# Weight sums by accumulating DMA: a later start in the unit table, oldest token first, the accumulation one loop turn behind its plain copy, and two GpSimd splits moved to VectorE

## The chip, the cores and the metric

The kernel runs on one core of one Trainium2 chip. The metric is device time in microseconds, from the first to the last instruction of the slowest core, here the only one. The profile is one execution of the same program, recorded by the hardware profiler.

## The reference, cut to what matters

One layer of a diffusion backbone, batch 1, 1024 latent tokens, width 1024, 256 context tokens. Two attention branches work on the same modulated tokens: A, windowed (each block of 128 queries sees at most 3 blocks of keys and the context, with a sink logit per head), and B, global (1024 + 256 keys). Each has 8 heads in 2 key groups. Their outputs are projected, gated, merged, and a ConvFFN follows:

```
proj = h @ w_in + b_in
o_a  = windowed_attention(q_a, k_a, v_a, k_ctx, v_ctx, sink)
o_b  = global_attention(q_b, [k_b, k_ctx], [v_b, v_ctx])
y    = (sigmoid(ga) * (o_a @ w_branch_a) + sigmoid(gb) * (o_b @ w_branch_b)) @ w_out
x    = layer_norm(alpha * x + gate1 * y)
u    = depthwise_conv3(h2 @ w_up)
y    = (silu(u_gate) * u_val) @ w_down
out  = layer_norm(alpha * x + gate2 * y)
```

The last product, with `w_down`, is done by a seven-product scheme on 2 x 2 blocks. It needs four sums of blocks of `w_down`, which are weights: they depend on nothing that the kernel computes.

## The kernel before, in words

Everything is float32 in two parts (a rounded high part and the rest), so a product is three matmuls (`mm3`, lines 88 to 91) or two where one operand is exact. The stages follow each other: modulation and projections, the gates, attention, merge and output projection with the first LayerNorm, the FFN up products, the down products with the second LayerNorm.

**Attention units.** The loop over `u` (0 to 32) goes over 32 units: units 0 to 15 are branch A (`br` 0), 16 to 31 are branch B (`br` 1). Unit `br_i_g` is query block `i` and key group `g`; tiles carry this in their names (`ptl_3_0_3` is of unit i=3, g=0). In a unit:

- `qprep` (two units ahead): GpSimd splits the queries into `qs` (lines 83, 86), TensorE transposes them (line 483), ScalarE copies to `q1`, and SyncE swaps halves by two DMAs `q<-q` (lines 487, 488).
- `lat`: TensorE makes the scores (lines 493, 494), VectorE `p` (line 538), ScalarE the exponential (line 505).
- `rows` (line 577 and after): the reciprocal row sums go to a small DRAM tile `dn` (DMA `dn<-rb`, line 586), and come back spread over partitions (two DMAs `rb<-dn`, line 588). The DRAM tag of each `dn` tile is put on a list, `tokens`.
- `tr_step`: TensorE transposes 128 x 512 of `p` to PSUM (`ptr`, line 614), ScalarE writes the high part `pth` (line 623), VectorE the low part `ptl` (line 624). For the key tiles in `POOL_LO` (tile 3 in branch A, 2 and 6 in B) the split is *pooled*: ScalarE copies `ptr` to `prw` (line 620), and GpSimd makes `pth` and `ptl` (lines 83, 86).
- `av_step`: two matmuls with `pth` and `ptl` (lines 635, 636).
- `out_step`: ScalarE copies `avs` (line 641), GpSimd `up` (line 643), VectorE or GpSimd `ot` (line 647), GpSimd multiplies by `rb` (line 650) and splits the result to `O` (lines 83, 86).

**The sums.** `DNS` (line 65) tells after which unit `wd_sums` is called, with which sum (`n`) and which blocks (`j0` to `j1`; 4, 4 and 3 of 11). Each call of `put` takes a tag from `tokens`, makes a DRAM tile `sd` with that tag, so that the tile's DMAs stand behind the `dn` tile that had the tag, fills it by a plain DMA on SyncE's queue (1 MB, or 768 KB for the last three blocks), and adds one more block by an accumulating DMA on GpSimd's queue (line 685). Sums 1 and 3 start from weights alone. Sum 2 starts as a copy of the finished sum 1, sum 4 as a copy of the finished sum 2. So a block group has 4 plain and 4 accumulating DMAs, and all three groups have 12 and 12.

**What sets the order.** In the attention stage no order is written out: a list scheduler with a cost model of its own emits each engine's instructions when their inputs and buffers are free, by the order of the program among those that are ready. An engine, SyncE and GpSimd among them, then works its list strictly in that order. A DMA instruction with a wait holds up all that stands behind it on its engine.

Of the kernel before, what the change touches and what calls it, by code (L numbers as in the profile page):

```python
# [10 lines left out]
ALU = mybir.AluOpType  # L11
# [7 lines left out]
NT = 8  # L19
# [9 lines left out]
POOL_LO = (3,), (2, 6)  # L29
# [32 lines left out]
VOFF = 0.0  # L62
VSPAN = 1.0
VSC = 0, 1
DNS = {u0 + 2 * n + (u0 == 20): (n, j0, j1) for u0, j0, j1 in ((16, 0, 4), (20, 4, 8), (24, 8, 11)) for n in range(3)}


@with_exitstack
def layer_kernel(
# [6 lines left out]
    nc = tc.nc  # L76
    PSUM = bass.MemoryType.PSUM

    def split(src, hi, lo, hi_eng, lo_eng):
        if hi_eng is nc.scalar:  # L80
            nc.scalar.copy(hi, src)  # L81
        elif hi_eng is nc.gpsimd:
            nc.gpsimd.tensor_scalar(out=hi, in0=src, scalar1=1.0, scalar2=0.0, op0=ALU.mult, op1=ALU.add)
        else:
            hi_eng.tensor_copy(hi, src)
        lo_eng.tensor_tensor(out=lo, in0=src, in1=hi.bitcast(F32), op=ALU.subtract)  # L86
# [376 lines left out]
    class Unit:  # L463
# [141 lines left out]
        def value_steps(self):  # L605
            nm, kt = self.id, self.kt
            vh = self.br * 2 + self.g
            last = self.id == f"1_{NT - 1}_1"
            parts = {}

            def tr_step(n):
                tr = pt_tile(f"ptr{nm}_{n}")
                for h in range(4):
                    nc.tensor.transpose(tr[:, h * P:(h + 1) * P], self.pslice(h, n), ident)  # L614
                hi = att.tile([P, 512], R32, tag="pth", name=f"pth{nm}_{n}", bufs=4)
                lo = att.tile([P, 512], R32, tag="ptl", name=f"ptl{nm}_{n}", bufs=4)
                pooled = n in POOL_LO[self.br] and not last
                if pooled:
                    rw = att.tile([P, 512], F32, tag="ptr", name=f"prw{nm}_{n}", bufs=2)
                    nc.scalar.copy(rw, tr)  # L620
                    split(rw, hi, lo, nc.gpsimd, nc.gpsimd)
                else:
                    nc.scalar.copy(hi, tr)  # L623
                    nc.vector.tensor_tensor(out=lo, in0=tr, in1=hi.bitcast(F32), op=ALU.subtract)  # L624
                parts[n] = hi, lo
                return pooled

            def av_step(n):
                first = self.left == len(kt)
                self.left -= 1  # L630
                if first:
                    self.av = ps2.tile([P, 512], F32, tag="av", name=f"av{nm}")
                hi, lo = parts.pop(n)
                v = VT[kt[n] // 2][:, kt[n] % 2, vh]
                nc.tensor.matmul(self.av, v, hi, start=first, stop=False)  # L635
                nc.tensor.matmul(self.av, v, lo, start=False, stop=self.left == 0)  # L636

            def out_step():
                av = self.av
                avs = att.tile([P, 512], F32, tag="ptr", name=f"avs{nm}", bufs=2)  # L640
                nc.scalar.copy(avs, av)  # L641
                up = att.tile([HD, 512], F32, tag="up", name=f"up{nm}", bufs=1)
                nc.gpsimd.tensor_scalar(out=up, in0=avs[HD:P], scalar1=1.0, scalar2=0.0, op0=ALU.mult, op1=ALU.add)
                ot = att.tile([P, 2, P], F32, tag="ot", name=f"ot{nm}", bufs=1)
                oe = nc.gpsimd if self.br and not last else nc.vector
                for h in range(2):
                    oe.tensor_tensor(out=ot[h * HD:(h + 1) * HD],
                                     in0=avs[0:HD].rearrange("p (a b q) -> p a b q", b=2, q=P)[:, :, h],
                                     in1=up.rearrange("p (a b q) -> p a b q", b=2, q=P)[:, :, h], op=ALU.add)
                nc.gpsimd.tensor_tensor(out=ot, in0=ot, in1=self.rb, op=ALU.mult)  # L650
                hf = self.i // 4
                qs = slice((self.i % 4) * P, (self.i % 4 + 1) * P)
                split(ot, otile(self.br, hf, 0, self.g)[:, :, qs], otile(self.br, hf, 1, self.g)[:, :, qs],
                      nc.gpsimd, nc.gpsimd)

            def step(ns):
                pooled = [tr_step(n) for n in ns]
                for n, pl in zip(ns, pooled):
                    clk[0] += 1
                    avq.append((self, n, clk[0] + LAG[self.br] + (PLAG[self.br] if pl else 0)))  # L660
                    av_issue()

            self.left = len(kt)
            self.av_step, self.out_step = av_step, out_step
            g = 1 + self.br
            steps = [lambda n=n: step(range(n, n + g)) for n in range(0, len(kt), g)]
            steps.insert(3 if self.br else 2 if self.i else len(steps), self.rows)
            return steps

    tokens = []  # L670
    sd = {}

    def wd_sums(n, j0, j1):
        def a(r, c):
            return w_dn[c * NH + j0:c * NH + j1][:, :, 4 * r:4 * r + 4].rearrange("n p f q -> p n (f q)")

        def put(key, src, *more):
            tag = tokens.pop()
            t = dpool.tile([P, j1 - j0, HALF], F32, tag=tag, name=f"sd{key}_{j0}")
            for j in range(j0, j1):  # L680
                sd[key, j] = t[:, j - j0]
            sd[key] = t
            nc.sync.dma_start(t, src)
            for m in more:
                nc.gpsimd.dma_start(t, m, accum_op=ALU.add)

        if n == 0:
            put(1, a(1, 0), a(1, 1))
            put(3, a(0, 0), a(1, 0))
        elif n == 1:  # L690
            put(2, sd[1], a(0, 0))
        else:
            put(4, sd[2], a(0, 1))
# [130 lines left out]
    for n, (gi, k) in enumerate(order):  # L824
# [8 lines left out]
        if gi == "g":  # L833
            for hf in (0, 1):
                last = gate(k, hf)
# [50 lines left out]
    def otile(br, hf, hl, g):  # L886
        key = br, hf, hl, g
        if key not in O:
            O[key] = opool.tile([P, 2, HALF], R32, tag="O", name="O%d%d%d%d" % key, bufs=12)
        return O[key]  # L890
# [4 lines left out]
    def pt_tile(name, dt=F32):  # L895
        return ps2.tile([P, 512], dt, tag="pt", name=name, bufs=3)
# [17 lines left out]
    def av_issue(flush=False):  # L914
        while avq:
            u = avq[0][0]
            c = [e for e in avq if e[0] is u and (flush or e[2] <= clk[0])]
            if not c:
                return
            e = min(c, key=lambda e: e[2])  # L920
            avq.remove(e)
            u.av_step(e[1])
            if u.left == 0:
                u.out_step()
# [36 lines left out]
    def done(br, i, g):  # L961
        if g and i % 2:
            hput(f"Q{br}_{i - 1}")
        if g and i == NT - 1:
            hput(f"KL{br * 2}", f"KL{br * 2 + 1}")
# [4 lines left out]
    for u in range(nu + 1):  # L970
        vs, fs = [], []
        while vq and (vq[0] <= u - VL or vq[0] >= 16 or u >= 17):
            vs += units[vq.pop(0)].value_steps()
        ss = []
        if u < nu:
            ss = units[u].score_steps()
            if u + 2 < nu:
                ss.append(units[u + 2].qprep)
        if u == 31:
            first = branch_steps(1, w_b, (0, 1), att, (nc.gpsimd, nc.gpsimd), (0,))  # L980
            first[0]()
        for hf, (u0, u1) in enumerate(FILL):
            if u == u0:
                fill += branch_steps(0, w_a, (hf,), att, (nc.gpsimd, nc.gpsimd))
                ends = [n * (u1 - u0) / len(fill) for n in range(len(fill))]
            if u0 <= u < u1:
                fs = [fill.pop(0) for e in ends if u - u0 <= e < u - u0 + 1]
        if u < nu:
            ss = [units[u].context] + ss
        seq = []  # L990
        for lst, of, sp in ((ss, 0.0, SPAN[u >= 17]), (vs, VOFF, VSPAN), (fs, 0.0, 1.0)):
            for n, st_ in enumerate(lst):
                seq.append((of + sp * (n + 0.5) / len(lst), st_))
        for _, st_ in sorted(seq, key=lambda e: e[0]):
            st_()
        if u in DNS:
            wd_sums(*DNS[u])
        if u < nu:
            vq.append(u)
            done(units[u].br, units[u].i, units[u].g)  # L1000
# [86 lines left out]
    for f in range(2, KT):  # L1087
# [4 lines left out]
        for hs in halves:  # L1092
            n = HALF * len(hs)
# [239 lines left out]
    for f in (4, 6):  # L1333
        for si in (1, 2):
# [3 lines left out]
            elif f == 6:  # L1338
                (_, st), (_, dg), (_, ca), *ap = ln1(si)
                n = len(pend) - 4  # L1340
# [584 lines left out]
```

## Time and profile before

| | us |
|---|---|
| median of 3 runs (1563.13 to 1565.62) | 1564.17 |
| the profiled execution | 1565.22 |
| its span, first to last instruction | 1563.4 |
| TensorE (PE) busy in the span | 1531.6 |
| VectorE (DVE), ScalarE (ACT), GpSimd (POOL) busy | 1187.6, 808.6, 782.2 |
| branch A units, about | 336 to 466 |
| branch B units, about | 458 to 756 |
| plain DMAs of the sums issued | 458.4 to 686.1 |
| accumulating DMAs of the sums issued | 465.7 to 692.3 |

In a row of the timeline the first number is the start in us from the span's start, the second the duration in us; a bracket at its end is the idle time of that engine just before, and what ended it. "POOL L685" is GpSimd's issue of an accumulating DMA, "SPq L683" SyncE's issue of a plain one. In a row of the windows view each engine's busy us in the stretch is followed by its number of instructions; then come the granted TensorE clock, the mean busy share of the 16 DMA engines, and GB/s.

### The profile page before, as it was taken

The numbers are of one execution on the slowest core, as the hardware profiler recorded it, in microseconds if no ns is written. First come the engines' busy times: TensorE is split into PE (matmuls) and PEld (weight loads), VectorE is DVE, ScalarE is ACT, GpSimd is POOL, SyncE is SP. The second block draws the span as 40 slices with busy tenths as digits, with TensorE's granted clock in tenths as the row PEclk, the third lists the DMA queues.
The fourth block names the chain that finished last, engine by engine and source line by source line (L and its number), as shares of the span: only waits on it lengthen the run. The fifth ranks groups of instructions, "written<-read, shape, count | busy, mean of one in ns | idle before, by whom it ended". The sixth has DMA issues, their size and how long they took to land.

```text
span 1563.4 us, 22286 instructions
## 1 busy us (share of the span) xinstructions
PE 1531.6 (98%) x7804; PEld 1282.2 (82%) x7804; DVE 1187.6 (76%) x1714; ACT 808.6 (52%) x1431; POOL 782.2 (50%) x795
## 2 busy tenths in 40 slices
PE   9999999999999999999999999999999999999997
PEld 7888888888877877877888997888888888888887
DVE  6677976548887777777774788888888888657884
ACT  5322223358887777777431673544444444435552
POOL 0356422526666777776332455666677764121121
PEclk9999999999999999999999999999999999999998
DMA  9776662322235666631550223233334446996721
GB/s 371 267 239 239 207 245 92 106 84 66 65 116 137 150 149 151 148 80 35 180 184 16 98 79 120 81 112 115 120 102 114 113 117 191 363 265 212 251 103 55
DMA packets 113105, 232.11 MB, mean 148 GB/s; under 512 B 13056, under 2 KB 27904, under 8 KB 112896
## 3 DMA queue, kind: packets, MB, share of 16 engines
q1 hardware_dynamic: 97760, 201.82, 38.4%
q0 software_dynamic: 10400, 20.19, 8.3%
q10 hardware_dynamic: 4832, 8.68, 1.5%
q8 instruction: 61, 1.00, 0.3%
q14 instruction: 52, 0.43, 0.1%
HBM read 179.45 MB, written 65.86 MB: 157 GB/s over the span
## 4 chain that ended last, share of the span: by engine, by line
PE 54%; DVE 3%; ACT 1%; issue 1%; POOL 0%; DVEq 0%; ACTq 0%
PE p L89 4%; PE p L90 4%; PE p L91 4%; PE b L89 2%; PE b L91 2%; PE b L90 2%; PE c L89 2%; PE c L91 2%; PE d L91 2%; PE d L89 2%; PE c L90 2%; PE d L90 2%; PE a L91 2%; PE a L89 2%; PE a L90 2%; PE y L91 2%
## 5 line engine op out<-in xcount | busy, mean ns | idle before, releaser
L624 DVE TENSOR_TENSOR ptl<-ptr,pth 128x512 fp32r<-128x512 f32 x190 | 126.2, 682 | 32.6 <-ACT pth L623 32.2
L623 ACT CAST pth<-ptr 128x512 fp32r<-128x512 f32 x190 | 108.0, 593 | 54.0 <-PE ptr L614 32.6
L86 DVE TENSOR_TENSOR ld<-rd,hd 128x1024 fp32r<-128x1024 f32 x77 | 94.9, 1249 | 50.2 <-ACT hd L81 48.1
L505 ACT ACTIVATE p<-p,nm 128x1024 f32<-128x1024 f32 (+2 forms) x128 | 125.9, 985 | 4.5 <-DVE p L538 4.3
L614 PE MATMUL ptr<-ident,p 128*128 128x128 f32 x816 | 122.4, 277 | 4.4 <-DVE ptl L624 3.2
L81 ACT CAST hd<-rd 128x1024 fp32r<-128x1024 f32 x77 | 79.5, 1050 | 81.1 <-PE p L91 55.1
L614 PEld LDWEIGHTS ptr<-ident,p 128*128 128x128 f32 x816 | 94.1, 141 | 25.6 <-DVE ptl L624 7.9
L86 POOL TENSOR_TENSOR wlg<-wg,whg 128x512 fp32r<-128x512 f32 x32 | 47.7, 1500 | 123.3 <-ACT whg L81 123.3
L635 PE MATMUL av<-pth,VT 128*128 128x512 f32 x236 | 104.6, 443 | 2.1 <-ACT avs L641 1.5
L89 PE MATMUL p<-hd 128*128 128x512 f32 x264 | 103.2, 391 | 0.0
L91 PE MATMUL p<-hd,ld 128*128 128x512 f32 x264 | 102.7, 389 | 0.0
L90 PE MATMUL p<-ld,hd 128*128 128x512 f32 x264 | 102.7, 389 | 0.0
L636 PE MATMUL av<-ptl,VT 128*128 128x512 f32 x236 | 98.1, 416 | 2.7 <-POOL ptl L86 2.7
L89 PE MATMUL g<-hh,whg 128*128 128x512 f32 x256 | 99.9, 390 | 0.0
L91 PE MATMUL g<-hh,wlg 128*128 128x512 f32 x256 | 99.7, 389 | 0.0
L90 PE MATMUL g<-hl,whg 128*128 128x512 f32 x256 | 99.6, 389 | 0.0
L538 DVE TENSOR_SCALAR_CACHE_REDUCE p<-s,cvt,nmc 128x1024 f32<-128x1024 f32 x64 | 83.2, 1316 | 8.8 <-PE s L494 7.7
L493 PE MATMUL s<-KL,q 128*128 128x512 f32 (+2 forms) x192 | 75.6, 394 | 5.3 <-ACT p_x L505 2.8
L787 ACT ACTIVATE sg<-g,bgc 128x512 f32<-128x512 f32 x32 | 22.0, 686 | 96.1 <-PE g L91 96.1
L494 PE MATMUL s<-KL,q 128*128 128x512 f32 (+2 forms) x192 | 71.6, 373 | 0.0
L81 ACT CAST wS<-s 128x512 fp32r<-128x512 f32 x76 | 45.3, 620 | 46.4 <-POOL s L1227 45.7
L81 ACT CAST wA<-ru 128x512 fp32r<-128x512 f32 x57 | 35.5, 623 | 62.4 <-PE d L91 33.8
(436 smaller groups left out, 5015.2 us busy)
## 6 DMA issues: line engine op xcount, KB each, us to landing
wml<-in_wmodT_dram SPq DMA_DIRECT2D x48, 512.0 KB
ru<-in_w_up_dram SPq DMA_DIRECT2D x38, 512.0 KB
rd<-td SPq DMA_DIRECT2D x55, 256.0 KB
rd<-sd SPq DMA_DIRECT2D x44, 256.0 KB
rd<-in_w_dn_dram SPq DMA_DIRECT2D x33, 256.0 KB
wm<-in_wmodT_dram SPq DMA_DIRECT2D x16, 512.0 KB
wg<-in_w_g_dram SPq DMA_DIRECT2D x32, 256.0 KB
sgd<-sg ACTq DMA_DIRECT2D x32, 256.0 KB
```

What stands on the lines that cost most here:

```text
L81: nc.scalar.copy(hi, src)
L86: lo_eng.tensor_tensor(out=lo, in0=src, in1=hi.bitcast(F32), op=ALU.subtract)
L89: nc.tensor.matmul(ps, a[0], b[0], start=start, stop=False, skip_group_check=resumed)
L90: nc.tensor.matmul(ps, a[0], b[1], start=False, stop=False, skip_group_check=resumed)
L91: nc.tensor.matmul(ps, a[1], b[0], start=False, stop=stop, skip_group_check=resumed)
L505: nc.scalar.activation(p, s, AF.Exp, bias=nm[:, h:h + 1], scale=scale, accum_out=sm[:, h:h + 1])
L538: nc.vector.tensor_scalar(out=p, in0=o, scalar1=self.qscale(nqs)[:, hs] if self.br else -1.0, scalar2=self.other[:, hs], op0=ALU.mult, op1 ...
L614: nc.tensor.transpose(tr[:, h * P:(h + 1) * P], self.pslice(h, n), ident)
L623: nc.scalar.copy(hi, tr)
L624: nc.vector.tensor_tensor(out=lo, in0=tr, in1=hi.bitcast(F32), op=ALU.subtract)
L635: nc.tensor.matmul(self.av, v, hi, start=first, stop=False)
L636: nc.tensor.matmul(self.av, v, lo, start=False, stop=self.left == 0)
```

## The change

Four edits:

```diff
-DNS = {u0 + 2 * n + (u0 == 20): (n, j0, j1) for u0, j0, j1 in ((16, 0, 4), (20, 4, 8), (24, 8, 11)) for n in range(3)}
+DNS = {u0 + 2 * n + (u0 == 22): (n, j0, j1) for u0, j0, j1 in ((18, 0, 4), (22, 4, 8), (26, 8, 11)) for n in range(3)}
...
-                pooled = n in POOL_LO[self.br] and not last
+                pooled = n in POOL_LO[self.br] and not last and self.id[:3] != f"0_{NT - 1}"
...
     tokens = []
+    adds = []
...
-            tag = tokens.pop()
+            tag = tokens.pop(0)
...
             nc.sync.dma_start(t, src)
-            for m in more:
-                nc.gpsimd.dma_start(t, m, accum_op=ALU.add)
+            adds.extend((t, m) for m in more)
...
         for _, st_ in sorted(seq, key=lambda e: e[0]):
             st_()
+        while adds:
+            t, m = adds.pop(0)
+            nc.gpsimd.dma_start(t, m, accum_op=ALU.add)
         if u in DNS:
             wd_sums(*DNS[u])
```

The table calls each sum two units later. The accumulating DMA of a sum stands in the program one turn of the unit loop behind its plain DMA. The tag is the oldest on the list and no longer the newest. And in units 0_7_0 and 0_7_1, the last two of the first branch, branch A, tile 3 is split by ScalarE and VectorE and not by GpSimd.

The table and the program say "later"; what the scheduler makes of it is another matter, since the newest token at unit 16 was that of a unit just done, and the oldest at unit 18 is that of unit 0. The first place is SyncE's list in the first units of branch A (`sd_0_6091` is sum 2 of the first blocks, `sd_0_6546` their sum 4, `dn` and `rb` the row sums, `q` the swapped queries, `bT` a gate load):

```order
+L684 DMA sd_0_6091<-sd_0_5615 16x16384
+L588 DMA rb_1_0_3386<-dn_1_0_3388 64x2x128 x2
 L586 DMA dn_1_1_3520<-rb_1_1_3518 4x128
+L487 DMA q_3_0_3570<-q_3_0_3569 64x512
 L588 DMA rb_1_1_3518<-dn_1_1_3520 64x2x128 x2
-L944 DMA bT_2_5946<-sgd_110 128x512
-L487 DMA q_3_0_3570<-q_3_0_3569 64x512
 L488 DMA q_3_0_3570<-q_3_0_3569 64x512
-L944 DMA bT_2_5946<-sgd_110 128x512
+L684 DMA sd_0_6546<-sd_0_6091 16x16384
 L586 DMA dn_2_0_3652<-rb_2_0_3650 4x128
```

Two plain DMAs of the sums, which copy a finished sum and so wait for an accumulation, now stand among the `dn`, `rb` and `q` DMAs of units 1_0 to 3_0 of branch A. All 12 plain DMAs stand between `dn` of unit 0_0 and `rb` of unit 5_1; before, the first stood behind `dn` of unit 7_0.

The second place is GpSimd's list in the same branch, where units 2_1 and 3_0 meet (`ot` and `O` are a unit's output, `pth` and `ptl` the pooled split, `qs` the split queries):

```order
+L650 TENSOR_TENSOR ot_2_1_3946<-ot_2_1_3946,rb_2_1_3782 128x256
 L83 TENSOR_SCALAR pth_3_0_3_3975<-prw_3_0_3_3977 128x512
-L650 TENSOR_TENSOR ot_2_1_3946<-ot_2_1_3946,rb_2_1_3782 128x256
+L83 TENSOR_SCALAR O_3449<-ot_2_1_3946 128x2x128
 L86 TENSOR_TENSOR ptl_3_0_3_3976<-prw_3_0_3_3977,pth_3_0_3_3975 128x512
-L83 TENSOR_SCALAR O_3449<-ot_2_1_3946 128x2x128
 L86 TENSOR_TENSOR O_3450<-ot_2_1_3946,O_3449 128x2x128
+L998 DMA sd_4_7235<-in_w_dn_dram 512x1x512
 L83 TENSOR_SCALAR qs_5_1_4221<-Q_4_1588 128x4x64
 L643 TENSOR_SCALAR up_3_0_4076<-avs_3_0_4074 64x512
```

An accumulating DMA, the seventh, now stands ahead of the query split and the pooled split of the next unit. There is one such row per unit from unit 0_0 on, 12 in all, the last behind `O` of unit 5_0.

The third place is where GpSimd came to the first sums before, at the end of branch A (`smc` and `p` of unit 0_0 are branch B's):

```order
 L86 TENSOR_TENSOR O_4481<-ot_6_1_5011,O_4480 128x2x128
-L685 DMA sd_0_5186<-in_w_dn_dram 512x1x512
-L83 TENSOR_SCALAR qs_1_1_5361<-Q_0_544 128x4x64
-L86 TENSOR_TENSOR qs_1_1_5361<-Q_0_544,qs_1_1_5361 128x4x64
-L83 TENSOR_SCALAR pth_7_1_3_5162<-prw_7_1_3_5164 128x512
-L86 TENSOR_TENSOR ptl_7_1_3_5163<-prw_7_1_3_5164,pth_7_1_3_5162 128x512
```

From here on the list held the 12 accumulating DMAs up to unit 5_1 of branch B; now it holds none, and the pooled split of the two last units of branch A is gone too.

## The prediction

> **What bounds the kernel now.** I read the page's head first.
>
> ```profile
> span 1563.4 us, 22286 instructions
> PE 1531.6 (98%) x7804; PEld 1282.2 (82%) x7804; DVE 1187.6 (76%) x1714; ACT 808.6 (52%) x1431; POOL 782.2 (50%) x795
> ```
>
> TensorE works 98% of the span. An edit to other engines' work can matter only where it makes or ends a wait of TensorE, or slows its clock. So next I read the windows view, cut in stretches around the attention stage.
>
> ```profile
> 345.00:440.00 95.00, 92.75 (x624) 80.24 (x623) 80.77 (x191) 81.80 (x193) 62.28 (x91) 1.00 0.26 68
> 450.00:465.00 15.00, 12.94 (x84) 10.47 (x83) 12.66 (x28) 12.89 (x35) 9.79 (x14) 1.00 0.50 159
> 465.00:480.00 15.00, 13.85 (x80) 11.08 (x79) 12.82 (x20) 13.09 (x31) 10.43 (x17) 1.00 0.87 200
> 480.00:495.00 15.00, 12.58 (x72) 10.09 (x71) 10.58 (x18) 8.36 (x18) 9.99 (x17) 0.89 0.51 100
> 495.00:750.00 255.00, 248.34 (x1428) 203.37 (x1428) 193.22 (x296) 188.31 (x408) 189.80 (x274) 1.00 0.48 116
> 458.00:700.00 242.00, 231.87 (x1329) 189.71 (x1330) 183.97 (x286) 180.44 (x398) 179.76 (x263) 0.99 0.59 139
> ```
>
> In branch A (345 to 440) TensorE is idle for 2.25 us of 95. Where the branches meet (450 to 495) it loses 2.06 + 1.15 + 2.42 = 5.63 us, and in the third window the clock is 0.89, which costs 0.11 x 15 = 1.65 us more. In branch B (495 to 750) it loses 6.66 us of 255. The timeline of TensorE names the waits at the meeting place.
>
> ```profile
> 464.63 0.50 PE L636 MATMUL av<-ptl,VT 128*128 128x512 f32 x1 [1.44 <-POOL ptl L86]
> 482.47 0.50 PE L636 MATMUL av<-ptl,VT 128*128 128x512 f32 x1 [0.62 <-POOL ptl L86]
> 484.77 1.64 PE L614 MATMUL ptr<-ident,p 128*128 128x128 f32 x8 [1.80 <-DVE ptl L624]
> 486.07 0.77 PE L635 MATMUL av<-pth,VT 128*128 128x512 f32 x1
> ```
>
> Right after the 1.80 us wait a matmul that took 0.50 us takes 0.77: the dip of the clock. GpSimd's timeline shows where the wait comes from, and SyncE's when that DMA's partner was issued.
>
> ```profile
> 466.28 0.61 SPq L683 DMA_DIRECT2D sd<-in_w_dn_dram  x1
> ...
> 477.40 1.18 POOL L685 DMA_DIRECT2D sd<-in_w_dn_dram  x1 [1.89 <-DMA sd<-in_w_dn_dram]
> 478.65 0.73 POOL L650 TENSOR_TENSOR ot<-ot,rb 128x256 f32<-128x256 f32 x1
> ...
> 482.50 0.61 POOL L643 TENSOR_SCALAR up<-avs 64x512 f32<-64x512 f32 x1
> ```
>
> GpSimd stood 1.89 us at an accumulating DMA until the plain one had landed, and `ot`, `O`, `ptl` and `up` came late behind it. So the sums do cost TensorE something where they are.
>
> **The change, part by part.** *The pooled pairs.* Units 0_7_0 and 0_7_1 lose two GpSimd splits, one of them the releaser of the 1.44 us wait. VectorE gets two `ptl` more:
>
> ```profile
> L624 DVE TENSOR_TENSOR ptl<-ptr,pth 128x512 fp32r<-128x512 f32 x190 | 126.2, 682 | 32.6 <-ACT pth L623 32.2
> ```
>
> That is 2 x 0.68 = 1.4 us on VectorE, which has 2.3 us free in its window (12.66 of 15). I cost it at nothing; without that cover it costs 1.4. ScalarE makes one copy either way.
>
> *The sums leave the end of branch A and branch B.* GpSimd is free of 12 issues and their waits there. At most this gives back all of 5.63 + 1.65 = 7.3 us at the meeting place, at least the 1.80 wait with its dip, 3.5. I take 6, nearest to the whole, since the two longest waits both lose their cause. In branch B the bounds are 0 and 6.66. I take 2, since no single wait there is put down to a sum.
>
> *The sums enter branch A.* The order shows that "two units later" is not what happens: the oldest token belongs to unit 0, and the 12 plain and 12 accumulating DMAs now stand in units 0_0 to 5_1, a pair per unit. The units there are short. Two neighbours on GpSimd's timeline give the pace, 397.26 - 389.06 = 8.20 us, and the rows behind give its slack.
>
> ```profile
> 389.06 0.74 POOL L86 TENSOR_TENSOR O<-ot,O 128x256 fp32r<-128x256 f32 x1
> ...
> 395.51 1.29 POOL L86 TENSOR_TENSOR ptl<-prw,pth 128x512 fp32r<-128x512 f32 x1
> ...
> 397.26 0.73 POOL L86 TENSOR_TENSOR O<-ot,O 128x256 fp32r<-128x256 f32 x1
> 399.45 0.41 POOL L83 TENSOR_SCALAR qs<-Q 128x256 fp32r<-128x256 f32 x1 [1.46 <-PE qtr L483]
> ...
> 402.42 0.62 POOL L83 TENSOR_SCALAR pth<-prw 128x512 fp32r<-128x512 f32 x1 [1.04 <-ACT prw L620]
> ```
>
> ```profile
> 397.42 0.47 PE L636 MATMUL av<-ptl,VT 128*128 128x512 f32 x1
> ```
>
> The seventh accumulating DMA stands right behind `O`, at 397.26 + 0.73 = 398.0. Behind it GpSimd idles 1.46 and 1.04 us before the next `pth`, and `ptl` is done (395.51 + 1.29 = 396.80) only 0.62 us before TensorE uses it. That is 3.1 us between this place and a wait of TensorE. The issue takes part of it:
>
> ```profile
> L685 POOL DMA_DIRECT2D sd<-in_w_dn_dram x12: 1085/1122/1375, 465.7 to 692.3; - x12
> DMA to landing us min/median/max: 7.4/9.1/13.2
> ```
>
> 1.12 us go to the issue, 2.0 are left. The waits decide. From issue to landing an accumulating DMA takes 9.1 us, 13.2 where a plain one runs beside it. For a plain one I take the place where GpSimd waited for it: 11.1 us in the rows above (466.28 to 477.40, beside an accumulating one), and 6.2 alone:
>
> ```profile
> 616.95 0.60 SPq L683 DMA_DIRECT2D sd<-in_w_dn_dram  x1
> ...
> 623.18 1.16 POOL L685 DMA_DIRECT2D sd<-in_w_dn_dram  x1 [1.74 <-DMA sd<-in_w_dn_dram]
> ```
>
> Now the chain, P for plain and A for accumulating, numbered in order. A1 needs P1; P3 copies what A1 finished; A3 needs P3; P4 needs A3; P5 is behind P4 on SyncE; A5, P7 (needs A5), A7 follow; later A11, P12, A12. Their places in the rows of before:
>
> ```profile
> 345.67 0.51 SPq L586 DMA_DIRECT2D dn<-rb  x1
> ...
> 369.43 0.59 SPq L488 DMA_DIRECT2D q<-q  x1
> ...
> 371.51 0.27 SPq L586 DMA_DIRECT2D dn<-rb  x1
> 373.71 1.29 SPq L588 DMA_DIRECT2D rb<-dn  x2
> ```
>
> ```profile
> 352.65 0.62 POOL L643 TENSOR_SCALAR up<-avs 64x512 f32<-64x512 f32 x1
> ```
>
> P1 can go at 346.2, A1 at 353.3 behind `up`. P4's place is 370.0, behind `q<-q`; `dn` of unit 2_0 (371.51), the next `q<-q` and P5 are queued behind it, and GpSimd's `ot`, the scores and A5 wait for those.
>
> Each transfer alone: A1 lands 362.4, P3 368.6, A3 377.7, so SyncE stands at P4 from 370.0 to 377.7. P4 lands 383.9, P5 goes 1.3 later (two `rb<-dn`) and lands 391.4, A5 400.5, P7 406.7. A7 starts at 406.7, its place was 398.0: 8.7 late. A11's place, ahead of the second part of `O`, is 397.26 + 4 x 8.20 = 430.1; with the delay 438.8, landed 447.9, and only then P12, landed 454.1. A12's place was 398.0 + 5 x 8.20 = 439.0: 15.1 us late.
>
> Each beside another where one is in flight: A1 lands 366.5, P3 377.6, A3 386.7 (SyncE stands, so alone), P4 392.9, P5 405.3, A5 418.5, P7 429.6, 31.6 late; A11 at 461.7 lands 470.8, P12 477.0: 38.0 late.
>
> A check by the DMA engines' share, from the windows of one plain and one accumulating DMA:
>
> ```profile
> 503.40:508.70 5.30, 5.30 (x35) 4.62 (x35) 3.94 (x8) 4.41 (x9) 4.25 (x9) 1.00 0.66 232
> 510.00:518.50 8.50, 8.50 (x47) 7.20 (x46) 5.67 (x9) 6.48 (x16) 3.95 (x5) 1.00 0.76 124
> ```
>
> 0.66 x 5.3 + 0.76 x 8.5 = 10 us of all 16 engines for a pair, 110 for 8 pairs of 1 MB and 4 of three quarters. From 346 to 439 are 93 us, and branch A uses 0.26 of them, 24. Less the last accumulation (6.5, behind A12's place): 127 us of work in 93, 34 late. By the long window of before, 0.59 x 242 - 0.26 x 242 = 80 for all sums, it is 98 in 93, 5 late. I take 25, about the middle of the chain's 15 and 38, inside the shares' 5 and 34. Less the slack of 2.0, TensorE loses 23 us (13 to 36).
>
> *Clock.* Such waits can bring dips like that at 486. Bounds: none, or one for each of six waits, 9.9 us; I take two, 3.3. The Trainium skill, "TensorE: Matmul & The Clock Gate", Part 1, halves the clock after an idle window of about 3.4 us. Here 0.62 and 1.80 us of waiting within 3 us sufficed, so by the trace shorter waits count too; by the page alone this term would go down to the waits over 3.4.
>
> *Sum.* 23 + 3.3 - 6 - 2 = 18.3. The profiled execution took 1565.2 (span and 1.8 around it), so 1583.5; the median of the runs is 1.05 below it. I predict 1583. The ends: 13 + 0 - 7.3 - 6.7 is about -1, 36 + 9.9 - 3.5 is +42.
>
> **The rivals.** *Faster: the transfers fit in branch A's idle DMA time.* The share there is 0.26, and GpSimd is idle in 32.7 us of 95. Lateness at A12 is 3A + 4P - 43.4 (at A7) plus A + P - 8.9 (at P12), so A and P 7% shorter than alone bring it from 15 to 10, where, without dips, 8 us of loss meet 8 of gain: that is the point from which it decides. With A at its least, 7.4, and P at 5.3, the whole of the window above, lateness is 3.8, TensorE loses 1.8, and with the whole gain the time is 1564.2 + 1.8 - 7.3 - 2 = 1557. For it: the 7.4 was seen. Against: half of the accumulations took 9.1 or more, and A2, A4 and A6 run beside the chain. The Trainium skill, "DMA: Bandwidth & Descriptors", section "Anatomy of one DMA", fits a GpSimd DMA as 2.0 us plus its bytes at 436 GB/s, an estimated 4.4 us for 1 MB; by that this rival would win. The trace's median of 9.1 disagrees.
>
> *About the same.* The chain with lone durations and no dip: 13 - 8 = +5, so 1569; with the whole gain of 7.3 and 6.7 at the other end, -1, so 1563.
>
> *Much slower: the DMA engines are full.* 34 late or more, six dips, gain only 3.5: 1564 + 42 = 1606.
>
> *The words hold* and the sums start at unit 18: 1557, as the first rival, since branch A stays as it is. The order speaks against it.
>
> **How the numbers follow.** Forecast (1572 to 1596 with a loss of 13 to 36 and the other terms as taken) 0.62; much slower 0.13; lone durations 0.13, half of it within 0.2%; faster 0.10; words hold 0.02. A measurement can tell 0.2%, 3.1 us, from no change. Faster 0.11, within 0.2% 0.08, slower 0.81. The range 1562 to 1603 leaves out the faster cases and about half of the much slower one.
>
> **What would show it.** In the profile after: POOL's accumulating DMAs between 353 and about 465, most with several us of idle before them, ended by a plain DMA; SyncE standing at P4, P7 and P12 for an accumulation; TensorE waiting for `ptl` or the scores in branch A, 20 us or so in all; a DMA share near 0.8 there; the waits at the meeting place shorter. I am wrong if TensorE is as busy in branch A as before (2.25 us idle of 95), or if accumulations land in under 8 us.

## The result, and the profile after

Before 1564.17 us (median of 5 runs), the changed kernel 1588.3 us (5 runs, 1587.52 to 1590.8). The ratio is 1.0159, with a 95% interval of 1.0145 to 1.0173: the change costs 24 us. The profiled execution took 1587.97 us, its span is 1586.2. The page's head of the changed kernel:

```profile
span 1586.2 us, 22269 instructions
PE 1540.6 (97%) x7804; PEld 1288.7 (81%) x7804; DVE 1193.9 (75%) x1716; ACT 808.0 (51%) x1431; POOL 783.9 (49%) x791
```

TensorE has the same 7804 instructions and is busy 9 us longer, though nothing was added to it. That is a first sign of a lower clock. The windows view of the changed kernel, then the one window of before that the prediction did not show; the last three columns are granted clock, DMA share and GB/s:

```profile
345.00:440.00 95.00, 76.27 (x466) 64.33 (x465) 65.12 (x145) 60.56 (x144) 55.05 (x74) 0.93 0.95 234
440.00:465.00 25.00, 23.10 (x152) 19.45 (x150) 20.55 (x47) 20.49 (x49) 20.84 (x28) 1.00 0.94 193
465.00:480.00 15.00, 11.75 (x66) 10.12 (x66) 10.35 (x24) 7.87 (x19) 7.03 (x10) 0.81 0.87 226
480.00:495.00 15.00, 14.65 (x95) 11.81 (x94) 12.05 (x27) 12.88 (x37) 8.63 (x14) 0.96 0.33 90
495.00:750.00 255.00, 250.07 (x1444) 205.73 (x1445) 197.29 (x310) 193.38 (x418) 178.39 (x267) 1.00 0.16 44
```

```profile
440.00:465.00 25.00, 22.85 (x154) 18.93 (x153) 21.46 (x51) 21.09 (x56) 15.69 (x23) 1.00 0.43 133
```

These rows give a ledger. What TensorE loses in a window is its idle time, plus the window times what is missing from a clock of 1.00.

| us lost by TensorE | before | after |
|---|---|---|
| idle, 345 to 480 | 2.25 + 2.15 + 1.15 = 5.55 | 18.73 + 1.90 + 3.25 = 23.88 |
| clock, 345 to 480 | 0 | 0.07 x 95 + 0.19 x 15 = 9.50 |
| 480 to 495, idle and clock | 2.42 + 1.65 = 4.07 | 0.35 + 0.60 = 0.95 |
| 495 to 750, idle | 6.66 | 4.93 |
| sum | 16.28 | 39.26 |

The difference, 22.98 us, is near that of the spans (1586.2 - 1563.4 = 22.8), so the change of time lies in these windows: 27.8 us lost before 480, 4.9 gained behind it. The clock's rows are a little too high. Of the 20.5 us at half speed before 482 us in the trace's clock records, 3.7 lie inside waits, where a slow clock costs nothing, and half of the other 16.8 is 8.4 us, against 10.1 in the rows (9.50 and 0.60).

The windows are fixed in time, and the work has moved under them. The first scores of branch B, before and after, show by how much:

```profile
457.91 0.39 PE L493 MATMUL s_x<-KC,q 128*128 128x256 f32 x1
```

```profile
488.99 0.39 PE L493 MATMUL s_x<-KC,q 128*128 128x256 f32 x1
```

Branch A ends 31.1 us later, near the 23.88 + 9.50 - 2.34 = 31.0 of the ledger (2.34 is the idle time of before that is branch A's own). GpSimd's third `smc`, in unit 1_0 of branch B, comes at 507.74 and 532.57, so 6.2 us are regained where the branches meet; the last `p_x` of branch B comes 23.8 us later than before, so 1.0 is regained in the rest of it.

TensorE's timeline in that stretch, the rows with the longest waits and one matmul after a short wait for comparison:

```profile
391.62 0.80 PE L635 MATMUL av<-pth,VT 128*128 128x512 f32 x1 [4.16 <-POOL pth L83]
397.93 0.50 PE L635 MATMUL av<-pth,VT 128*128 128x512 f32 x1 [0.34 <-ACT avs L641]
405.89 0.29 PE L577 MATMUL str<-ident,sm 128*4 128x128 f32 x1 [3.68 <-DVE ptl L624]
426.64 0.69 PE L493 MATMUL s<-KL,q 128*128 128x384 f32 x1 [2.65 <-DVE p L538]
475.12 1.11 PE L614 MATMUL ptr<-ident,p 128*128 128x128 f32 x4 [2.67 <-DVE p L538]
```

The same `av` matmul takes 0.80 us right after 4.16 us of waiting and 0.50 six us later. At each of the four long waits here a stretch of lower clock begins, before or just after the wait's end (in the trace's clock records at 388.9, 406.0, 426.5 and 474.3 us; the first and last 6.83 us long, the others 3.41, 20.5 us of half speed in all).

Behind the 4.16 stands GpSimd. Its timeline, rows of the accumulating DMAs only, and their landing times:

```profile
389.05 1.17 POOL L998 DMA_DIRECT2D sd<-in_w_dn_dram  x1 [7.15 <-DMA sd<-sd]
402.05 1.18 POOL L998 DMA_DIRECT2D sd<-in_w_dn_dram  x1 [8.21 <-DMA sd<-in_w_dn_dram]
420.76 1.18 POOL L998 DMA_DIRECT2D sd<-in_w_dn_dram  x1 [4.66 <-DMA sd<-sd]
```

```profile
L998 POOL DMA_DIRECT2D sd<-in_w_dn_dram x12: 1141/1177/1381, 354.1 to 469.4; - x12
DMA to landing us min/median/max: 7.8/11.4/12.8
```

GpSimd stands up to 8 us at one accumulating DMA for its plain one, and the pooled split behind it comes late. Its waits for plain DMAs between 345 and 470 (us in total, times, longest), those that copy a finished sum first:

```profile
POOL sd L998 <- DMA sd<-sd: 20.7, 5, 7.2
POOL sd L998 <- DMA sd<-in_w_dn_dram: 11.7, 2, 8.2
```

The seventh accumulating DMA (A7) is at 420.76, and the twelfth (A12) at 469.4, 30.4 us behind its place. SyncE's timeline shows the fourth, seventh and twelfth plain DMA (P4, P7, P12), which copy a finished sum:

```profile
382.93 0.53 SPq L684 DMA_DIRECT2D sd<-sd  x1
...
413.38 0.53 SPq L684 DMA_DIRECT2D sd<-sd  x1
...
464.45 0.51 SPq L684 DMA_DIRECT2D sd<-sd  x1
```

They were issued within 0.02 us of the landing of A3, A5 and A11 in the trace (382.92, 413.37, 464.44). In all, SyncE stands 24.3 us for accumulations between 345 and 470:

```profile
SPq L684 <- DMA sd<-in_w_dn_dram: 24.3, 4, 7.4
```

One more thing shows in SyncE's waits there. The first row is of before, the second of after:

```profile
SPq L588 <- DMA dn<-rb: 13.2, 14, 1.9
```

```profile
SPq L588 <- DMA dn<-rb: 26.9, 10, 4.6
```

The write of the row sums, 2 KB, has no part in the sums, but where SyncE waited 0.9 us for it (13.2 / 14), it now waits 2.7 (26.9 / 10). The small DMAs come late among the large ones. Worked out from the completions in the trace, the query swap `q<-q` (line 487) lands a median of 2.3 us after its issue between 345 and 465 before, and 5.8 after.

### The profile page after: what moved, and what is told of

It is laid out like the page before. It is cut to its first block, busy times and chain, and to the rows that moved or that the text cites. A ratio compares the mean times of both kernels' runs of the same rounds, so it can differ in the third digit from the quotient of the medians.

```text
span 1586.2 us, 22269 instructions
## 1 busy us (share of the span) xinstructions
PE 1540.6 (97%) x7804; PEld 1288.7 (81%) x7804; DVE 1193.9 (75%) x1716; ACT 808.0 (51%) x1431; POOL 783.9 (49%) x791
## 4 chain that ended last, share of the span: by engine, by line
PE 54%; DVE 3%; ACT 1%; issue 1%; POOL 0%; DVEq 0%; ACTq 0%
PE p L91 4%; PE p L90 4%; PE p L89 4%; PE b L89 2%; PE b L90 2%; PE b L91 2%; PE c L89 2%; PE d L89 2%; PE c L90 2%; PE c L91 2%; PE d L91 2%; PE d L90 2%; PE a L89 2%; PE a L91 2%; PE a L90 2%; PE y L89 2%
```

## The experiments

Theory A in what follows is the prediction's chain: SyncE and GpSimd stand for one transfer after another. Theory B is its check: the DMA engines have about as much to move in branch A as they can. The common rival is that not the place of the sums, but the table, the deferral or the un-pooled splits cost the time by the order that they give the engines. Times are medians; ratios are to the kernel before on the same chip, with 95% intervals.

### Place or program order: one edit at a time

**The newest tag again** in the changed kernel:

```diff
-            tag = tokens.pop(0)
+            tag = tokens.pop()
```

> The changed kernel with one edit: the tag is the newest on the list again. Theory (the loss is the place of the sums in branch A, where one pair of 1 MB DMAs per 8.2 us unit fills the DMA engines and SyncE's and GpSimd's queues): the sums now stand in branch B, a pair per unit of about 17 us, and the whole loss goes; 1561 us (1556 to 1566), TensorE idle about 2 us between 345 and 440 as before. Rival (the deferred accumulation, the later table or the un-pooled splits cost it by the order they give the engines): those three stay, so 1580 or more.

Measured 1558.69 us, ratio 0.9971 (0.9961 to 0.9982). One word takes back the whole loss and 5 us more. This version beats both kernels. Its windows of branch A, of the place where the branches meet, and of branch B:

```profile
345.00:440.00 95.00, 92.53 (x621) 80.18 (x620) 81.35 (x191) 81.70 (x192) 62.17 (x91) 1.00 0.26 68
440.00:465.00 25.00, 24.10 (x159) 19.65 (x158) 21.81 (x52) 21.05 (x56) 14.54 (x22) 1.00 0.33 91
465.00:480.00 15.00, 14.03 (x82) 11.15 (x81) 13.37 (x25) 14.59 (x34) 8.39 (x16) 1.00 0.23 62
480.00:495.00 15.00, 14.92 (x93) 12.09 (x91) 12.67 (x21) 13.45 (x30) 11.97 (x19) 1.00 0.59 140
495.00:750.00 255.00, 248.59 (x1439) 204.61 (x1438) 194.18 (x298) 185.27 (x398) 190.48 (x275) 1.00 0.54 126
```

Branch A runs as before. Where the branches meet there is no dip of the clock (with the un-pooled splits alone, below, there is none there either), and 1.05 us of idle time from 465 to 495 in place of 3.57. Branch B carries all the sums and is no worse than before (idle 6.41 of 255).

**The oldest tag alone** in the kernel before:

```diff
-            tag = tokens.pop()
+            tag = tokens.pop(0)
```

> The kernel before with one edit: the tag is the oldest on the list. Theory (place in branch A): the sums stand in units 0_0 to 5_1 of branch A as in the changed kernel, TensorE falls back by 25 to 32 us there, the meeting place gives back 4 to 6; 1588 us (1583 to 1595). Rival (order of the code: table, deferral, un-pooled splits): none of these is made, so 1564.

Measured 1594.26 us, ratio 1.0199 (1.0185 to 1.0213). The tag alone makes the loss, and more of it than the whole change.

**The un-pooled splits alone** in the kernel before:

```diff
-                pooled = n in POOL_LO[self.br] and not last
+                pooled = n in POOL_LO[self.br] and not last and self.id[:3] != f"0_{NT - 1}"
```

> The kernel before with one edit: tile 3 of units 0_7_0 and 0_7_1 is split by ScalarE and VectorE. Theory: the 1.44 us wait of TensorE for GpSimd's ptl goes, nothing else does; 1563 us (1560.5 to 1564.5). Rival (VectorE's 1.4 us more lies in TensorE's way): 1565.5 or more.

Measured 1562.22 us, ratio 0.9991 (0.9983 to 1.0). The medians differ by 1.9 us, and the interval goes from nothing to 2.7; VectorE's extra work does not show.

**The oldest tag and the un-pooled splits**, table and place of the accumulating DMA as before:

> The kernel before with the oldest tag and the un-pooled splits; the table and the place of the accumulating DMA in the program as before. Every engine's list reads like the changed kernel's. Theory (under the oldest tag the table and the deferral change nothing, and the 6 us between the oldest tag alone, 1594.3, and the changed kernel, 1588.3, are the two pooled splits): 1588.3 us (1586 to 1590.5). Rival (the 6 us are not the splits but the later table or the deferral, by way of something that the lists don't show, such as where the DRAM tiles lie): 1594 us (1592 to 1596).

Measured 1590.7 us, ratio 1.0173 (1.0159 to 1.0187). It lies between the two forecasts, nearer to the theory's. Of the 6 us between 1594.3 and 1588.3 the two splits take 3.6. Why that is more than the 1.9 of the splits alone was not tested; that GpSimd is late here is a likely reason. The other 2.4 are not explained, and the interval overlaps that of the changed kernel, so that they may be nothing. They are not the order of the code: in the two traces every engine's list is the same from end to end (by line and tile name, buffer numbers left out). So under the oldest tag the table and the deferral change no list at all.

**The newest tag without the deferral**, which leaves of the change the later table and the un-pooled splits (besides the tag's edit, as above):

```diff
-            adds.extend((t, m) for m in more)
+            for m in more:
+                nc.gpsimd.dma_start(t, m, accum_op=ALU.add)
```

> The changed kernel with the newest tag and the accumulating DMA issued right behind its plain one again, so of the change only the later table and the un-pooled splits are left. Theory (the 3.5 us between the un-pooled splits alone, 1562.2, and all but the oldest tag, 1558.7, come from the table, which moves the first pairs away from where the branches meet): 1558.7 us (1557 to 1560.5). Rival (they come from the deferral, which keeps GpSimd from standing at a sum for its plain copy): 1561 us or more.

Measured 1559.78 us, ratio 0.9976 (0.9967 to 0.9985). That is 2.4 us under the un-pooled splits alone and 1.1 over the version with the deferral. The intervals overlap on both sides, so the times do not settle how much the table brings. The window from 480 to 495, of the un-pooled splits alone and then of this kernel, shows what it does:

```profile
480.00:495.00 15.00, 11.84 (x78) 9.69 (x76) 11.14 (x20) 10.11 (x23) 10.25 (x18) 1.00 0.51 96
```

```profile
480.00:495.00 15.00, 14.92 (x93) 12.17 (x92) 12.67 (x21) 13.31 (x30) 11.94 (x19) 1.00 0.61 144
```

The table alone takes TensorE's idle time there from 3.16 us to 0.08, and it is 0.08 with the deferral too. It moves the first plain DMA of the sums from 458.6 us to 482.1.

### No sums at all

The changed kernel takes weight blocks where the sums stood:

```diff
-            t = dpool.tile([P, j1 - j0, HALF], F32, tag=tag, name=f"sd{key}_{j0}")
+            t = src
...
-            nc.sync.dma_start(t, src)
-            adds.extend((t, m) for m in more)
```

> The changed kernel without the 24 DMAs of the sums: the down products take the first weight block of each sum in place of the sum, so the third operand of the scheme is wrong in value and its loads are as long. Theory (all of the loss, and some of the time before, is the sums' DMAs): branch A runs as before, the meeting place and branch B without their waits for a sum, so 1556 us (1551 to 1560): the sums cost 8 us before and 31 in the changed kernel. Rival (order of the code): 1580 or more, since table and un-pooled splits cost it.

Measured 1557.78 us, ratio 0.9962 (0.9949 to 0.9976). Against it the kernel before is 6.4 us slower (1564.14 on this chip). This kernel has the un-pooled splits too, so the sums' DMAs cost about 4.4 of that (1562.22 with these splits alone). They cost 30.5 in the changed kernel and 0.9 with the newest tag, where the intervals overlap. So that version has almost nothing left to gain from moving them.

### Chain or transfers

**No chain.** Sums 2 and 4 start from weights:

```diff
-            put(2, sd[1], a(0, 0))
+            put(2, a(1, 0), a(0, 0))
-            put(4, sd[2], a(0, 1))
+            put(4, a(1, 0), a(0, 1))
```

> The changed kernel, where sums 2 and 4 start from a weight block and not from the finished sum 1 or 2 (as many bytes, the value of these two sums is wrong): no plain DMA waits for an accumulation any more. Theory A (the chain of waits sets the lateness: SyncE stands at the fourth, seventh and twelfth plain DMA): the accumulations wait only for their own plain one, TensorE loses under 10 us in branch A; 1567 us (1560 to 1574). Theory B (the DMA engines are full: 98 to 127 us of transfers in 93): nothing is taken off them, the loss stays; 1586 us (1580 to 1592) and a DMA share of 0.9 or more between 345 and 465.

Measured 1584.05 us, ratio 1.0129 (1.0116 to 1.0143): only 4 us less. Theory A, as the only cause, falls. Windows of this kernel, then one row each of the waits of GpSimd, SyncE and TensorE (whose largest is 8.9 us for `p`):

```profile
345.00:440.00 95.00, 78.55 (x496) 66.52 (x495) 66.84 (x149) 64.25 (x151) 58.95 (x80) 0.96 0.99 242
440.00:465.00 25.00, 20.67 (x127) 17.41 (x126) 20.12 (x46) 17.33 (x41) 17.80 (x24) 0.92 1.03 231
```

```profile
POOL sd L998 <- DMA sd<-in_w_dn_dram: 19.9, 4, 7.3
```

```profile
SPq L588 <- DMA dn<-rb: 41.9, 13, 6.8
```

```profile
PE s L494 <- DMA q<-q: 4.1, 4, 1.4
```

SyncE no longer stands for a sum. GpSimd still stands 19.9 us where it stood 32.4, now only for plain DMAs that are slow to land, and SyncE 41.9 us for the little `dn`. The DMA share is 0.99 and 1.03 (a share over 1 cannot be exact): full.

**Small accumulations**, 1/32 of the bytes, with all waits:

```diff
-            nc.gpsimd.dma_start(t, m, accum_op=ALU.add)
+            nc.gpsimd.dma_start(t[0:4], m[0:4], accum_op=ALU.add)
```

> The changed kernel, where each accumulating DMA adds 4 of the 128 partitions (1/32 of the bytes; the sums are wrong): all waits and their order stay. By theory A the chain at the seventh accumulation is 3 x 3 + 4 x 5.5 = 31 us against 43.4 of place, by theory B the transfers are 11 x 3.5 + 24 = 63 us in 93: both expect no loss in branch A, 1560 us (1556 to 1565). Rival (issues and in-order waits in a short unit cost it whatever the bytes): 1575 or more.

Measured 1561.57 us, ratio 0.9983 (0.9974 to 0.9992). The window of branch A and the landing times:

```profile
345.00:440.00 95.00, 89.94 (x594) 76.87 (x593) 81.83 (x184) 77.64 (x184) 68.37 (x98) 1.00 0.62 183
```

```profile
DMA to landing us min/median/max: 2.9/3.8/5.9
```

With the same 24 DMAs and the same waits, the loss is down to 4 us above no sums. The 3 us for a small accumulation in the forecast had no run behind it; the median is 3.8. Both theories expected no loss in branch A; the rival, that issues and in-order waits cost it whatever the bytes, falls.

**Half of the bytes**, `t[0:64]` and `m[0:64]` in the same line:

> The changed kernel, where each accumulating DMA adds 64 of the 128 partitions (half of its bytes; the sums are wrong): order and waits as in the changed kernel. Theory B (the transfers' time against the 93 us of the stretch, a threshold): 11 x 3.5 + 11 x 3.25 + 24 = 98 us, 5 us over, less the slack of 2, so about 1558 + 3 = 1562 us (1560 to 1568), a DMA share of 0.85 or more but few waits. Rival (a loss in proportion to the bytes, from 1561.6 with 1/32 to 1588.3 with all): 1575 us (1571 to 1579).

Measured 1570.64 us, ratio 1.0048 (1.0034 to 1.0062): 9.1 us above the small accumulations, where all bytes cost 26.7. Neither forecast holds, since it is more than the threshold gave and just under the range for a loss in proportion.

```profile
345.00:440.00 95.00, 83.77 (x528) 70.91 (x527) 74.14 (x162) 69.01 (x163) 62.81 (x88) 0.96 0.82 209
```

```profile
DMA to landing us min/median/max: 5.1/6.9/9.1
```

**A pair every second unit**, all bytes:

```diff
-    adds = []
+    adds, used = [], []
...
-            tag = tokens.pop(0)
+            tag = tokens.pop(len(used))
+            used.append(tag)
```

> The changed kernel with the tags of units 0, 2, 4 and so on instead of 0, 1, 2: a pair of DMAs every second unit, eight in branch A and four at its end and in branch B. Both theories: a pair's 10 us of DMA time and the chain of about 9 + 6 us per step fit into 16.4 us; TensorE loses under 5 us in branch A, the meeting place keeps part of its waits; 1562 us (1557 to 1568). Rival (any sum in a short unit costs about 2 us, as 31 over 12 now): 1557 + 8 x 2 = 1573 or more.

Measured 1560.46 us, ratio 0.9976 (0.9966 to 0.9985), with this window:

```profile
345.00:440.00 95.00, 91.40 (x606) 78.07 (x605) 79.57 (x186) 79.21 (x189) 67.55 (x95) 1.00 0.82 190
```

Set beside the half bytes, this is the sharpest pair of the study. The DMA share in branch A is 0.82 in both, yet TensorE is idle 3.6 us here and 11.2 there (in an execution that is 3.8 us slower than the median of that kernel, so some of the 11.2 may be its own). So the share alone does not decide. Theory B as a plain threshold falls as well. A likely reason is that with a pair in every unit each delay meets the next pair, while with every second unit free the queues catch up. No run shows this by itself, and this edit gives the chain more time too, so the pair does not tell the chain from the transfers.

**Plain DMAs on GpSimd's queue**, so that SyncE never stands for a sum:

```diff
-            nc.sync.dma_start(t, src)
+            nc.gpsimd.dma_start(t, src)
```

> The changed kernel with the plain DMAs on GpSimd's queue: SyncE never stands for a sum, GpSimd stands for the plain ones' landing and for the chain. Theory A1 (SyncE's standing, which holds back the row sums and the swapped queries, is what TensorE pays): most goes, 1568 us (1560 to 1575). Theory A2 (GpSimd's standing is what it pays): no less than now, 1590 us (1585 to 1605). Theory B (full DMA engines): 1588 us (1583 to 1595).

Measured 1596.2 us, ratio 1.0209 (1.0193 to 1.0225). So theory A1, that SyncE's standing is what TensorE pays, falls. A2's range holds the result, and B's misses it by 1 us; the run does not tell these two apart. The largest wait of TensorE between 345 and 475 is now this:

```profile
PE s L494 <- DMA q<-q: 20.0, 6, 7.4
```

The swapped queries come late, though their queue carries no sum. In the changed kernel the same wait is 2.2 us. It is the landing that is late: by the trace's completions, two of these waits (3.95 us to 437.92, 2.58 us to 450.44) ended as the second swap (line 488) landed, 7.0 and 10.1 us after its issue; before, that swap took 3.9 us at most between 345 and 465.

**Traffic that nobody waits for**, three plain DMAs a pair on three queues, no sums:

```diff
-            t = dpool.tile([P, j1 - j0, HALF], F32, tag=tag, name=f"sd{key}_{j0}")
+            t = src
+            cp = dpool.tile([3, P, j1 - j0, HALF], F32, tag=tag, name=f"cp{key}_{j0}")
+            for k, q in enumerate((nc.sync, nc.gpsimd, nc.scalar)):
+                q.dma_start(cp[k], a(1, 0))
...
-            nc.sync.dma_start(t, src)
-            adds.extend((t, m) for m in more)
```

> No sums at all, but as much traffic in branch A: each put issues three plain DMAs of a weight block (1 MB, or 768 KB) into a DRAM tile that nobody reads, one each on SyncE's, GpSimd's and ScalarE's queue, behind the same tags; the down products take weight blocks in place of the sums (values wrong). Nobody waits for a sum or for one of these DMAs. Theory B1 (full DMA engines slow the row sums' and queries' small DMAs, and that alone stops TensorE): 3 x 3.5 us a pair as now, the loss stays in the main, 1578 us (1570 to 1592). Theory B2 (full DMA engines count only because SyncE and GpSimd stand for the sums' own landing): 1562 us (1557 to 1568), with a DMA share of 0.9 and small DMAs landing late all the same.

Measured 1613.27 us, ratio 1.0318 (1.0304 to 1.0332), far beyond both forecasts: 55 us more than without any traffic. TensorE's largest wait in the same stretch, and the window:

```profile
PE s L494 <- DMA q<-q: 28.8, 7, 7.4
```

```profile
345.00:440.00 95.00, 70.35 (x405) 58.77 (x403) 59.09 (x128) 54.71 (x127) 47.41 (x67) 0.87 0.80 274
```

The scores wait for `q<-q`, which lands a median of 7.6 us after its issue here (from the trace's completions, as above). So traffic whose result no engine needs is enough to stop TensorE, with two limits: the waits of SyncE still name these DMAs,

```profile
SPq L683 <- DMA cp<-in_w_dn_dram: 8.5, 2, 5.3
...
SPq L588 <- DMA cp<-in_w_dn_dram: 6.0, 1, 6.0
```

14.5 us of standing that the edit was meant to avoid; and the size does not carry over, since the traffic was matched by DMA time and moves 33 MB where the sums move 22 (274 GB/s against 234).

## Why the prediction was right, and where it was off

- **The sums leave for branch A, not "two units later".** Right: 12 accumulating DMAs from 354.1 to 469.4, and the tag alone does it (1564.1 to 1594.3 in the kernel before, 1588.3 back to 1558.7 in the changed one).
- **The waiting in branch A**, 23 us forecast. The changed kernel idles 23.88 us from 345 to 480, before 5.55, of which 2.06 + 1.15 belong to the meeting place, which the prediction books apart: 23.88 - 2.34 = 21.5. Right in size. The places were inside the bounds: P4 at 382.93 (377.7 to 386.7), A7 at 420.76 (406.7 to 429.6), P12 at 464.45 (447.9 to 470.8), A12 at 469.4 (454.1 to 477.0). A12 is 30.4 us late, 25 was taken. By the prediction's own rule, lateness less 2.0 of slack, 30.4 would give 28.4 us of waiting and not 21.5, and most of the loss stays without the chain (below). So the near hit of this term is in part luck.
- **The prices of the chain.** The 6.2 us taken for a plain DMA alone are those of a 768 KB one, up to GpSimd's next start; by the completions of before, P1 and P3, 1 MB each, landed 5.4 and 5.3 us after their issue. With 5.4 the chain's lower end is 11.1 us late, not 15.1. The 7.4 of the faster rival was a 768 KB accumulation as well; the fastest of 1 MB took 8.8 us before.
- **The clock**, 3.3 us forecast (two dips). This is the term that was mis-sized: 9.5 us by the ledger, near the bound of 9.9, and still 8.4 without the half speed that lies inside waits. There were four dips, not two, and two of them lasted twice as long. The waits at them were 4.16, 3.68, 2.65 and 2.67 us; the first dip began 1.5 us into its wait. The Trainium skill, "TensorE: Matmul & The Clock Gate", Part 1, asks for an idle window of about 3.4 us; two of these four waits are shorter, so the trace still does not agree with a bound that strict. The 5.1 us (8.4) to 6.2 us (9.5) by which the term was short are more than the 4.7 that the sum was off by.
- **The meeting place**, 6 us gained. The loss there was 2.06 + 1.15 + 4.07 = 7.28, and the changed kernel loses 0.95 in its window from 480 to 495: 6.3. That window is still branch A in the changed kernel, but read by the work (first `s_x` to third `smc`) the gain is 6.2. Right. Part of it are the un-pooled splits (1.9 us alone, 3.6 with the oldest tag), which the prediction did not price apart.
- **Branch B**, 2 us gained. 6.66 - 4.93 = 1.7 by the windows, 1.0 by the work. Right in size.
- **The sum.** 21.5 + 9.5 - 6.3 - 1.7 = 23.0, where 18.3 was forecast: 6.2 more by the clock, 1.5 less by the waits. (The prediction's own figures, 1583.5 less 1.05, give 1582.5 and not 1583.)
- **The mechanism.** The prediction put the loss down to a chain of waits and used the DMA share as a check. The runs show that the two are not one cause and its check. Without the chain, 1584.05 - 1558.69 = 25.4 of the 29.6 us between the changed kernel and the newest tag remain, with the DMA engines full. With all bytes at half the pace, 1.8 remain (1560.46). So the prediction was right on the place and near on the size, and gave too much weight to the chain. The loss needs the bytes and the pace: a pair that takes about 8 us of all DMA engines, beside the units' own small DMAs, in every unit of 8.2 us. (The sums' time: 0.95 x 95 + 0.94 x 25 + 0.87 x 15 = 126.8 us of all engines from 345 to 480, less 0.26 x 95 + 0.33 x 25 + 0.23 x 15 = 36.4 that the version with the newest tag uses there, is 90.4, or 8.2 for each of 11 pairs of 1 MB; 10 and 7.3 were the estimates.)
- **Landing times.** "Accumulations land in under 8 us" would have made it wrong: the median is 11.4. One of the 12 took 7.8, a 768 KB one near the end; the fastest of 1 MB took 9.7.
- **A DMA share near 0.8** was forecast in branch A: 0.95.
- **"The words hold", 1557 us.** The rival's price was right for a kernel that does what the words say: with the newest tag it is 1558.7.

What stays open: how much of the changed kernel's loss each late transfer brings (GpSimd's `pth`, `s` behind `p`, `q<-q`), since a delay in one passes to the others; why the oldest tag with the splits, with the same lists, is 2.4 us slower than the changed kernel, if it is; and what the clock alone costs, since no run kept the clock up with the waits in place.

## What to carry to other kernels

Where a buffer's tag decides when a scheduler may start a DMA, look first which tag is taken. Under the oldest tag the table of "when" changed no engine's list; under the newest it moved the first sum by 23.5 us. Background transfers need a place where a pair takes well under the time of a unit: the same bytes cost 0.9 us in the long units of branch B, 2.7 in every second unit of 8 us, and 30 in each of them. When pricing waits of TensorE, price the clock with them: four waits, 13.2 us together, took 8 to 10 us more by the clock.

## What the runs showed of the hardware

- The DMA share of a stretch is no measure of the harm by itself: at 0.82 TensorE idled 3.6 us of 95 in one kernel and 11.2 in another.
- Large transfers between DRAM tiles delay small ones, on other queues too: SyncE's wait for a 2 KB write rose from 0.9 us a time to 2.7 and, without the chain, 3.2 (41.9 / 13); with all sums on GpSimd's queue TensorE waited 20.0 us for `q<-q` on SyncE's, with two that landed 7.0 and 10.1 us after their issue against 3.9 at most before.
- The accumulating DMAs landed in 11.4 us among others (eight of 1 MB, four of 768 KB), with half of the bytes in 6.9, with 1/32 in 3.8 (medians).
- Plain traffic with no reader, 274 GB/s at a DMA share of 0.80, cost 55 us, the sums 30.5 at 0.95 and 234 GB/s.
- In the clock records of the changed kernel a dip within the attention stage is half speed for 3.41 or 6.83 us. Dips began at waits of TensorE of 4.16, 3.68, 2.65 and 2.67 us, and none at the pair of 2.26 and 1.08 us that ended at 377.36.
